# The order of the output projection's three parts, and where the last cached latents and the value weights are held, in a two-layer hybrid trunk

## The chip, the cores and the metric

The kernel runs on one core of one Trainium2 chip. The metric is the device time of one execution in microseconds (us), the median of several runs. The profile is of one further execution.

## The reference, cut to what matters

Two layers, each a SwiGLU, a mixer with three kinds of heads, and a second SwiGLU. 256 prompt tokens and 8 sample sequences of 8 new tokens go through together: 320 columns.

```python
x = x + 0.5 * swiglu(rms_norm(x, W['norm_ffn1'][l]), W['ffn1_wi'][l], W['ffn1_wo'][l])
p = rms_norm(x, W['norm_mix'][l]) @ W['w_in'][l]
...
o_hg, hg_s = hgrn2_mixer(p_hg, lbs[l], W['hg_norm'][l], hg_s0[l])
o_rw, rw_s, rw_sh = rwkv7_mixer(p_rw, rw_sh0[l], rw_s0[l], l, W)
o_mla = attend(l, q_nope, q_pe, c, k_pe)
o = jnp.concatenate([o_hg, o_rw, o_mla], axis=-1)      # 256 + 256 + 512 columns
x = x + o @ W['w_out'][l]
x = x + 0.5 * swiglu(rms_norm(x, W['norm_ffn2'][l]), W['ffn2_wi'][l], W['ffn2_wo'][l])
...
# the MLA attention of the samples, over 2048 cached positions in 16 pages of 128
s_past = jnp.einsum('bqhr,bkr->bhqk', q_lat, c_past) + jnp.einsum('bqhe,bke->bhqk', q_pe, kpe_past)
pr = jax.nn.softmax(s, axis=-1)
o_lat = jnp.einsum('bhqk,bkr->bqhr', pr[..., :P], c_past) + jnp.einsum('bhqk,bkr->bqhr', pr[..., P:], c)
o = jnp.einsum('bqhr,rhd->bqhd', o_lat, wuv)
```

## The kernel before, in words

Activations lie transposed: 128 features on the partitions, 320 tokens along a row, eight such tiles for the 1024 features (`xT`, and `oh`/`ol` for the mixer's output). Every dense product is made with operands split into a high and a low part (`split`: a cast on ACT, a subtraction on DVE) and three matmuls for each 128 x 128 block of weights (`block`, `dense`). Weights of the mixer come as a stream `wm` of chunks of four blocks in the order of their use; `_pack_mixer` lays them out by `OUT_PARTS`, so the stream follows any change of it. Four chunks can wait as loaded (`raw`), three as split (`w4`).

The mixer of a layer is written as generators that `weave` interleaves: `hg` (HGRN2), `prompt` (attention of the prompt), `sample` (attention of the samples), `w_out` (parts of the output projection). A generator yields the estimated time after which it may go on, or the name of an event that it waits for; `weave` keeps an estimate of PE's time (`self.pe`). This gives the order in which the program is written. A planner then lists the instructions of each engine and queue in order of time by its own costs, earlier instructions first where several are ready; `issue_after(i)` keeps an instruction behind `i` on its engine. On the chip every engine goes through its list in order.

`sample` handles the eight sequences in four pairs p. For each pair, `scores` multiplies queries with key pages (tag `ct`, five places of two pages), `values` multiplies the soft-max with latent pages (tag `cn`, five places of two pages) in four chunks of two halves (`hf`) of two sequences (`si`). While pair p has its values made, pair p+1 has its scores made; in the last pair (p = 3) there are values alone. Pages are loaded from SP's queue, one transfer of 128 KB for each. Then come the product with the new keys, the division by the sum (L988), two transposes, the copy into `qlat` (L994), and the product with the value weights `wuv`, which are loaded into two places of `cn` (L1000).

The output projection adds its result to `xT` (L613, L625) for eight column blocks m, part by part. `w_out` makes the parts [2, 3] (RWKV-7; waits for R0 and R1) and [4, 5] (half of MLA; waits for the end of `sample` and of `prompt`) within `weave`, and `mix_out` the last, [6, 7, 0, 1], after it, where each column block is followed by its share of the next norm. L293 is the line of all matmuls but transposes (L297), L434 and L435 the two instructions of every split.

Of the kernel before, what the change touches and what calls it, by code (L numbers as in the profile page):

```python
# [20 lines left out]
TP = 256  # L21
# [5 lines left out]
RANK = 256  # L27
# [11 lines left out]
LEVELS = [32, 16, 8, 4, 2, 1]  # L39
PACE = (0, 1.05)  # L40
ORDER_A = lambda fill, sample: (sample, fill)
ORDER_B = lambda prompt, sample: (sample, prompt)

LAG = 2.8
# [12 lines left out]
def _blocks(w):  # L57
    k, n = w.shape
    return w.reshape(k // 128, 128, n // 128, 128).transpose(2, 0, 1, 3).reshape(-1, 128, 128)
# [2 lines left out]
RW_TILES = [6, 2, 0, 4, 3, 1, 5]  # L62
HG_TILES = [2, 0, 4, 6, 3, 1, 5, 7]

OUT_PARTS = [(("R0", "R1"), [2, 3]), (("smp", "prompt"), [4, 5]), (None, [6, 7, 0, 1])]


def _perm(tiles):
    return np.concatenate([np.arange(j * 128, j * 128 + 128) for j in tiles])


def _stream(parts, n):
    b = np.concatenate(parts, 0)
    return b.reshape(-1, n, 128, 128).transpose(0, 2, 1, 3).reshape(-1, 128, n * 128)


def _pairs(b, K):

    return b.reshape(-1, 2, K // MBLK, MBLK, 128, 128).transpose(0, 2, 1, 3, 4, 5).reshape(-1, 128, 128)
# [7 lines left out]
def _pack_mixer(i, l):  # L87
# [10 lines left out]
    return _stream([_pairs(_blocks(mlt[:, :256]), KD), _blocks(mlt[:, 256:]), _blocks(qq), np.zeros((QPAD, 128, 128), wo.dtype), _blocks(rw[:, _perm(RW_TILES)]), _blocks(hg[:, _perm(HG_TILES)]),  # L98
                    *[_blocks(np.concatenate([wo[r * 128:r * 128 + 128] for r in p], 0)) for _, p in OUT_PARTS]], MBLK)

# [163 lines left out]
class Kern:  # L264
# [339 lines left out]
    def w_out(self):  # L604
        for wait, part in OUT_PARTS[:-1]:
            for e in wait:
                yield e
            ohs, ols = [self.oh[:, k, :] for k in part], [self.ol[:, k, :] for k in part]
            for m in range(KD):
                self.mark(f"w_out{self.l}")  # L610
                po = self.bank()[:, :T]
                yield from self.dense_steps(po, len(part), ohs, ols)
                self.nc.vector.tensor_tensor(out=self.xT[:, m, :], in0=po, in1=self.xT[:, m, :], op=ALU.add)  # L613
                if len(part) == 1:
                    yield 0

    def mix_out(self, l, fp, nxt):
        self.mark(f"mix_out{l}")
        part = OUT_PARTS[-1][1]
        ohs, ols = [self.oh[:, k, :] for k in part], [self.ol[:, k, :] for k in part]  # L620
# [230 lines left out]
    def sample(self):  # L851
        nc, l = self.nc, self.l
# [4 lines left out]
        ps = self.bank("pa")  # L857
# [3 lines left out]
        qlat = self.qlat  # L861
# [4 lines left out]
        def ready(name, n):  # L866
            f = feed[name]
            f[0] = max(f[0], f[1][f[2] - 3] if f[2] > 2 else 0.0) + n * (PACE[1] if f[2] < PACE[0] else 1.05)
            f[2] += 1
            return 0, f[0] + 2.2  # L870

        def pages(i, n):

            with self.tc.issue_after(self.gat[-8].ins) if len(self.gat) >= 8 else ExitStack():
                return nc.values_load_multi_w_load_instructions(
                    self.pti[0:1, i:i + n], engines=[mybir.EngineType.SP], min_val=0, max_val=NPOOL - 1,
                    skip_runtime_bounds_check_because="a page table names pages of the pool")[1]
# [44 lines left out]
        def exps(p, ch):  # L922
            m = mx[p]
            nc.scalar.activation(S[p, ch], S[p, ch], AF.Exp, bias=m[:, 5:6], scale=MLA_SCALE, accum_out=m[:, ch:ch + 1])  # L924

        def values(p, ch, po):
            r0 = ready("cn", 4)
            cns_ = []
            rs = []
            for si in range(2):  # L930
                i = (2 * p + si) * NPAGE + ch * 4
                rs.append(pages(i, 4))
            for hf in range(2):
                for si in range(2):
                    cn = self.s([128, 2, RANK], "cn", 5)
                    for pg in range(2):
                        r = rs[si][hf * 2 + pg]
                        self.gat.append(nc.sync.dma_start(cn[:, pg, :], self.ap["cn"][l, bass.ds(r, 1)].rearrange("a p c -> p (a c)")))
                    cns_.append(cn)
            yield 0, r0[1] - 1.5  # L940
            self.mark(f"sample{l}")
            if ch < 3:
                exps(p, ch + 1)
            pt = self.bank("pa")
            for pg in range(4):
                self.tr(pt[:, pg * 128:pg * 128 + 128], S[p, ch][:, pg * 128:pg * 128 + 128], idt)
            PT = self.s([128, 512], "PT", 2)
            nc.vector.tensor_copy(PT, pt)
            yield 0, max(self.pe + 1.2, r0[1])
            for hf in range(2):  # L950
                self.mark(f"sample{l}")
                for pg in (2 * hf, 2 * hf + 1):
                    for si in range(2):
                        self.mm(po[64 * si:64 * si + 64, :RANK], PT[:, pg * 128 + 64 * si:pg * 128 + 64 * si + 64],
                                cns_[2 * hf + si][:, pg % 2, :], start=ch == 0 and pg == 0, stop=False)
                feed["cn"][1].append(self.pe)
                if hf == 0:
                    yield ready("cn", 4)
# [4 lines left out]
        soft(0)  # L963
        yield 2.0
        for p in range(4):
            po = self.bank("pv")
            exps(p, 0)
            for ch in range(4):
                yield from values(p, ch, po)
                if p < 3:  # L970
                    yield from scores(p + 1, ch)
            exps(p, 4)
            nc.vector.tensor_reduce(out=mx[p][:, 6:7], in_=mx[p][:, 0:5], axis=AX.X, op=ALU.add)
            nc.vector.reciprocal(mx[p][:, 6:7], mx[p][:, 6:7])
            yield 0.6
            self.mark(f"sample{l}")
            pt = self.bank("pa")
            self.tr(pt[:64, :128], S[p, 4], idt)
            PN = self.s([64, 128], "PT", 2)
            nc.vector.tensor_copy(PN, pt[:64, :128])  # L980
            if p < 3:
                soft(p + 1)
            yield 0.8
            self.mark(f"sample{l}")
            for si in range(2):
                self.mm(po[64 * si:64 * si + 64, :RANK], PN[:, 64 * si:64 * si + 64], cns, start=False, stop=True)
            ol = self.s([128, RANK], "PT", 2)
            nc.vector.tensor_scalar(out=ol, in0=po[:, :RANK], scalar1=mx[p][:, 6:7], scalar2=None, op0=ALU.mult)  # L988
            yield 0.9
            self.mark(f"sample{l}")  # L990
            pt = self.bank("pa")
            for rt in range(2):
                self.tr(pt[:, rt * 128:rt * 128 + 128], ol[:, rt * 128:rt * 128 + 128], idt)
            nc.scalar.copy(qlat[:, 0:2, 2 * p:2 * p + 2, :, :].rearrange("p r s h t -> p r (s h t)"),  # L994
                           pt[:, :256].rearrange("p (r x) -> p r x", r=2))
            yield 2.0
        self.mark(f"sample{l}")
        wuv = [self.s([128, 512], "cn", 5) for rt in range(2)]
        for rt in range(2):
            nc.sync.dma_start(wuv[rt], self.ap["wuv"][l][:, rt * 512:rt * 512 + 512])  # L1000
        yield 4.0
        self.mark(f"sample{l}")
        for g in range(4):
            ps = self.bank("pa")
            for rt in range(2):
                for hh in range(2):
                    h = 2 * g + hh
                    self.mm(ps[64 * hh:64 * hh + 64, :64], wuv[rt][:, h * 64:h * 64 + 64], qlat[:, rt, :, h, :],
                            start=rt == 0, stop=rt == 1)
            self.split(ps[:, :64], self.oh[:, 4 + g, TP:], self.ol[:, 4 + g, TP:])  # L1010
        self.ev["smp"] = self.pe + 1.0


# [542 lines left out]
```

## Time and profile before

| | |
|---|---|
| median of 3 runs | 1659.08 us (1657.40 to 1660.34) |
| the profiled execution, its own time | 1657.07 us |
| span of its profile | 1655.1 us |
| busy: PE, its weight loads, DVE, ACT, POOL | 98%, 87%, 58%, 43%, 5% |
| mean granted clock | 0.993 |
| DMA | 260.82 MB, mean 158 GB/s |

The span runs from the first to the last instruction of the profile. Busy time is the union of an engine's instructions; a line of the timeline merges neighbours of a kind (xcount). An arrow in brackets gives the idle time just before and what ended it. The last pair's values and the end of the mixer lie at 550 to 606 us in layer 0 and at 1367 to 1420 us in layer 1.

### The profile page before, as it was taken

What the parts mean: (1) busy time and instruction counts of PE and PEld (TensorE: products, weight loads), DVE (VectorE), ACT (ScalarE), POOL (GpSimd) and SP (SyncE); (2) the same over time, 40 slices, a digit from 0 to 9 for tenths busy, and PEclk for the clock granted to TensorE, in tenths of its full rate; (3) what the DMA queues carried; (4) which work ended last, traced back from release to release, by engine and by line L of the source; (5) the groups of instructions that cost most, each with busy time, mean ns of one, the idle gap of its engine ahead of it and who ended that gap; (6) DMA issues with size and microseconds to landing.
All of it is one profiled execution on the core that took longest, in us unless ns stands there. A gap on an engine that the chain in (4) does not pass through costs nothing.

```text
span 1655.1 us, 33369 instructions
## 1 busy us (share of the span) xinstructions
PE 1615.0 (98%) x13138; PEld 1441.2 (87%) x13138; DVE 957.8 (58%) x1593; ACT 716.0 (43%) x1207; POOL 83.6 (5%) x118
## 2 busy tenths in 40 slices
PE   8999999999999899999999999999999999999998
PEld 8999998776657599999999999987766676999997
DVE  7555448853445585555465554479444665755543
ACT  6444434543353364444344443346333534544432
POOL 0000000200022000000000000012000310000000
PEclk9999999999999999999999999999999999999999
DMA  8444536646673464445445544365457644454442
GB/s 284 148 149 150 153 90 183 179 134 193 182 219 91 143 215 146 150 153 149 147 149 153 148 147 152 100 187 178 118 173 212 205 134 147 151 149 153 153 146 90
DMA packets 131899, 260.82 MB, mean 158 GB/s; under 512 B 17872, under 2 KB 76816, under 8 KB 131744
## 3 DMA queue, kind: packets, MB, share of 16 engines
q1 hardware_dynamic: 118912, 237.34, 47.5%
q10 hardware_dynamic: 12800, 21.30, 4.3%
q8 instruction: 103, 1.69, 0.4%
q0 software_dynamic: 32, 0.07, 0.1%
q14 instruction: 52, 0.43, 0.1%
HBM read 253.52 MB, written 4.47 MB: 156 GB/s over the span
## 4 chain that ended last, share of the span: by engine, by line
PE 88%; DVE 5%; ACT 3%; DMA 2%; issue 1%; SPq 1%; ACTq 0%; DVEq 0%
PE pd L293 33%; PE pr L293 31%; PE pa L293 18%; PE pv L293 4%; DVE w L435 1%; PE pa L297 1%; ACT S L924 1%; DMA cn<-in_cn 1%; DMA raw<-in_wm 1%; DMA ct<-in_ct 1%; DMA xT<-in_x 0%; DVE kS L458 0%; ACT w L434 0%; DVE rt L1073 0%; ACT L924 0%
## 5 line engine op out<-in xcount | busy, mean ns | idle before, releaser
L435 DVE TENSOR_TENSOR w<-raw,w 128x1024 fp32r<-128x1024 f32 (+1 forms) x390 | 412.6, 1060 | 320.1 <-ACT w L434 313.4
L434 ACT CAST w<-raw 128x1024 fp32r<-128x1024 f32 (+1 forms) x390 | 353.2, 910 | 420.5 <-PE pd L293 192.4
L293 PE MATMUL pd<-xh,w 128*128 128x320 f32 x1792 | 423.7, 316 | 8.3 <-ACT w L434 7.1
L293 PEld LDWEIGHTS pd<-xh,w 128*128 128x128 f32 x1792 | 305.2, 189 | 25.5 <-issue 11.4
L293 PE MATMUL pd<-xl,w 128*128 128x320 f32 x896 | 279.9, 314 | 0.0
L293 PE MATMUL pr<-xh,w 128*128 128x320 f32 x1056 | 240.2, 310 | 0.0
L293 PE MATMUL pa<-xh,w 128*128 128x320 f32 x896 | 201.7, 309 | 0.0
L293 PEld LDWEIGHTS pr<-xh,w 128*128 128x128 f32 x1056 | 178.3, 188 | 0.5
L293 PEld LDWEIGHTS pd<-xl,w 128*128 128x128 f32 x896 | 169.7, 189 | 4.9 <-issue 3.5
L293 PE MATMUL pr<-xl,w 128*128 128x320 f32 x528 | 162.5, 309 | 0.0
L293 PE MATMUL pd<-hh,w 128*128 128x320 f32 x704 | 158.2, 309 | 0.0
L293 PE MATMUL pr<-hh,w 128*128 128x320 f32 x704 | 158.2, 309 | 0.0
L293 PEld LDWEIGHTS pa<-xh,w 128*128 128x128 f32 x896 | 151.0, 188 | 0.0
L293 PE MATMUL pa<-xl,w 128*128 128x320 f32 x448 | 137.6, 309 | 0.0
L293 PE MATMUL pa<-ct,qlat 96*64 96x256 f32 x768 | 122.4, 391 | 2.6 <-ACT qlat L994 1.8
L293 PEld LDWEIGHTS pr<-hh,w 128*128 128x128 f32 x704 | 118.4, 188 | 0.0
L293 PEld LDWEIGHTS pd<-hh,w 128*128 128x128 f32 x704 | 118.4, 188 | 0.0
L293 PE MATMUL pr<-hl,w 128*128 128x320 f32 x352 | 108.8, 309 | 0.0
L293 PE MATMUL pd<-hl,w 128*128 128x320 f32 x352 | 108.8, 309 | 0.0
L482 ACT ACTIVATE fa<-fa 128x320 f32<-128x320 f32 x88 | 41.4, 472 | 134.7 <-DVE fa L481 134.7
L293 PEld LDWEIGHTS pr<-xl,w 128*128 128x128 f32 x528 | 99.1, 188 | 0.3
L293 PEld LDWEIGHTS pa<-ct,qlat 96*64 96x64 f32 x768 | 60.6, 137 | 38.4 <-issue 12.2
(388 smaller groups left out, 1996.6 us busy)
## 6 DMA issues: line engine op xcount, KB each, us to landing
raw<-in_wf SPq DMA_DIRECT2D x264, 512.0 KB, 3.6
ct<-in_ct SPq DMA_DIRECT2D x256, 144.0 KB, 3.0
cn<-in_cn SPq DMA_DIRECT2D x256, 128.0 KB, 2.3
raw<-in_wm ACTq DMA_DIRECT2D x76, 256.0 KB, 3.1
raw<-in_wm SPq DMA_DIRECT2D x50, 256.0 KB, 3.5
xT<-in_x SPq DMA_DIRECT2D x4, 320.0 KB, 6.8
wukt<-in_wukt SPq DMA_DIRECT2D x2, 576.0 KB, 5.5
S<-in_rws SPq DMA_DIRECT2D x4, 256.0 KB, 2.9
```

What stands on the lines that cost most here:

```text
L293: self.last = self.nc.tensor.matmul(out, w, x, start=start, stop=stop)
L297: self.nc.tensor.transpose(out, x, ident)
L434: self.cast = nc.scalar.copy(h, src).ins
L435: nc.vector.tensor_tensor(out=lo, in0=src, in1=h.bitcast(F32), op=ALU.subtract)
L482: nc.scalar.activation(a, a, AF.Silu)
L924: nc.scalar.activation(S[p, ch], S[p, ch], AF.Exp, bias=m[:, 5:6], scale=MLA_SCALE, accum_out=m[:, ch:ch + 1])
```

## The change

`OUT_PARTS` becomes [2, 3], [0, 1], and last [4, 5, 6, 7]. The second part waits for the events of both HGRN2 halves and for "end", which is set as the last half of the last values is written; its matmuls are kept behind the last value product (`self.held`). In the last pair the second half of each chunk loads its latents into places of `ct`, and so does `wuv`, which is asked for at the start of that pair. The four groups of the final sample product share one PSUM bank and one split.

```diff
-OUT_PARTS = [(("R0", "R1"), [2, 3]), (("smp", "prompt"), [4, 5]), (None, [6, 7, 0, 1])]
+OUT_PARTS = [(("R0", "R1"), [2, 3]), (("h0", "h1", "end"), [0, 1]), (None, [4, 5, 6, 7])]
...
             for m in range(KD):
                 self.mark(f"w_out{self.l}")
                 po = self.bank()[:, :T]
-                yield from self.dense_steps(po, len(part), ohs, ols)
+                with self.tc.issue_after(self.held) if "end" in wait else ExitStack():
+                    self.dense(po, len(part), ohs, ols)
+                yield 0
                 self.nc.vector.tensor_tensor(out=self.xT[:, m, :], in0=po, in1=self.xT[:, m, :], op=ALU.add)
-                if len(part) == 1:
-                    yield 0
...
-                    cn = self.s([128, 2, RANK], "cn", 5)
+                    cn = self.s([128, 2, RANK], "ct" if p == 3 and hf else "cn", 5)
...
                 self.mark(f"sample{l}")
+                if (p, ch, hf) == (3, 3, 1):
+                    self.ev["end"] = self.pe
                 for pg in (2 * hf, 2 * hf + 1):
...
+                self.held = self.last.ins
...
         for p in range(4):
+            if p == 3:
+                wuv = [self.s([128, 512], "ct", 5) for rt in range(2)]
+                for rt in range(2):
+                    nc.sync.dma_start(wuv[rt], self.ap["wuv"][l][:, rt * 512:rt * 512 + 512])
             po = self.bank("pv")
...
-        wuv = [self.s([128, 512], "cn", 5) for rt in range(2)]
-        for rt in range(2):
-            nc.sync.dma_start(wuv[rt], self.ap["wuv"][l][:, rt * 512:rt * 512 + 512])
-        yield 4.0
-        self.mark(f"sample{l}")
+        ps = self.bank("pa")
         for g in range(4):
-            ps = self.bank("pa")
             for rt in range(2):
                 for hh in range(2):
                     h = 2 * g + hh
-                    self.mm(ps[64 * hh:64 * hh + 64, :64], wuv[rt][:, h * 64:h * 64 + 64], qlat[:, rt, :, h, :],
+                    self.mm(ps[64 * hh:64 * hh + 64, g * 64:g * 64 + 64], wuv[rt][:, h * 64:h * 64 + 64], qlat[:, rt, :, h, :],
                             start=rt == 0, stop=rt == 1)
-            self.split(ps[:, :64], self.oh[:, 4 + g, TP:], self.ol[:, 4 + g, TP:])
+        self.split(ps[:, :256].rearrange("p (g t) -> p g t", g=4), self.oh[:, 4:8, TP:], self.ol[:, 4:8, TP:])
```

## Rows read from the trace of the kernel before

**Rows 1.** The page: span, and busy time of the engines.
```profile
span 1655.1 us, 33369 instructions
...
PE 1615.0 (98%) x13138; PEld 1441.2 (87%) x13138; DVE 957.8 (58%) x1593; ACT 716.0 (43%) x1207; POOL 83.6 (5%) x118
```

**Rows 2.** Windows: length, busy PE, PEld, DVE, ACT, POOL; clock, DMA share, GB/s.
```profile
545.00:550.00 5.00, 3.95 (x28) 2.72 (x24) 4.89 (x15) 4.38 (x11) 0.00 (x0) 1.00 0.50 151
...
1360.00:1365.00 5.00, 3.60 (x32) 2.57 (x30) 4.51 (x15) 2.66 (x6) 0.00 (x0) 1.00 0.64 179
```

**Rows 3.** Windows, end of the samples in layer 0, layer 1, and after it.
```profile
550.90:562.60 11.70, 11.69 (x79) 6.70 (x80) 6.61 (x17) 5.23 (x20) 0.00 (x0) 1.00 0.59 165
562.60:570.90 8.30, 6.13 (x44) 3.08 (x42) 2.56 (x9) 1.69 (x5) 0.00 (x0) 1.00 0.59 182
570.90:574.00 3.10, 2.05 (x22) 1.26 (x22) 0.53 (x2) 0.58 (x2) 0.00 (x0) 0.83 0.00 0
574.00:576.30 2.30, 2.30 (x15) 1.95 (x14) 0.40 (x2) 0.21 (x1) 0.00 (x0) 0.50 0.00 0
...
1379.60:1385.90 6.30, 5.27 (x35) 2.39 (x33) 2.38 (x8) 1.33 (x3) 0.00 (x0) 1.00 0.64 206
1385.90:1388.70 2.80, 1.67 (x23) 0.84 (x23) 0.53 (x2) 0.64 (x3) 0.00 (x0) 1.00 0.00 0
...
582.90:606.00 23.10, 23.10 (x158) 22.94 (x158) 20.24 (x38) 15.91 (x29) 0.00 (x0) 1.00 0.76 261
```

**Rows 4.** Timeline of PE, layer 0: start, us, instruction, count, idle before.
```profile
550.91 1.95 PE L293 MATMUL pv<-cn,PT 128*64 128x256 f32 x16
...
564.50 0.65 PE L293 MATMUL pv<-cn,PT 128*64 128x256 f32 x4 [0.52 <-DMA cn<-in_cn]
...
568.06 0.82 PE L293 MATMUL pd<-pPT,V 128*64 128x256 f32 x8
570.25 0.65 PE L293 MATMUL pv<-cn,PT 128*64 128x256 f32 x2 [1.37 <-DMA cn<-in_cn]
...
572.06 0.44 PE L297 MATMUL pa<-cf,PT 128*128 128x128 f32 x2 [0.59 <-DVE PT L988]
572.96 1.12 PE L293 MATMUL pa<-qlat,cn 128*64 128x64 f32 x16 [0.46 <-ACT qlat L994]
```

**Rows 5.** Timeline of PE, layer 1.
```profile
1380.63 1.26 PE L293 MATMUL pv<-cn,PT 128*64 128x256 f32 x6 [0.48 <-DMA cn<-in_cn]
...
1385.20 0.65 PE L293 MATMUL pv<-cn,PT 128*64 128x256 f32 x2 [0.55 <-DMA cn<-in_cn]
```

**Rows 6.** Timeline of SP's queue, layer 0, and its longest wait for the values.
```profile
540.00 4.50 SPq L938 DMA_DIRECT2D cn<-in_cn  x8
...
552.02 13.11 SPq L938 DMA_DIRECT2D cn<-in_cn  x21
565.23 0.85 SPq L1000 DMA_DIRECT2D cn<-in_wuv  x2
566.27 0.34 SPq L938 DMA_DIRECT2D cn<-in_cn  x1
...
SPq L938 <- PE pv L293: 12.1, 5, 6.9
```

**Rows 7.** The chain that ended last: 48 dense matmuls in a row (start, us).
```profile
25.27 7.04 PE pa L293 x48
```

**Rows 8.** Timelines of ACT and DVE at the samples' end; HGRN2's last splits.
```profile
572.54 0.37 ACT L994 COPY qlat<-pa 128x256 f32<-128x256 f32 x1 [3.23 <-PE pa L297]
...
571.52 0.48 DVE L988 TENSOR_SCALAR PT<-pv,smx 128x256 f32<-128x256 f32 x1 [1.76 <-PE pv L293]
...
569.34 0.42 DVE L435 TENSOR_TENSOR xl<-pd,xh 128x256 fp32r<-128x256 f32 x1 [1.26 <-ACT xh L434]
...
547.10 0.47 DVE L435 TENSOR_TENSOR xl<-EX,xh 128x320 fp32r<-128x320 f32 x1
```

**Rows 9.** Transfers into `cn` between 505 and 575.
```profile
DMA to landing us min/median/max: 1.9/2.1/3.9
```

## The prediction

> **What bounds the kernel now.** The page comes first: TensorE (PE) is busy for 1615.0 of a span of 1655.1 us [rows 1]. An edit is therefore worth what it changes in PE's 40 us without work, in the granted clock, or in the number of matmuls. This change leaves the matmuls as they are. Second, the windows, to find the idle time: the reader is to see that each layer has two thin places at the end of its mixer. The earlier one [rows 2] lies before the first values of the last sample pair, and nothing in the change touches the soft-max it waits for. The later one is where the change works [rows 3]: from 562.6 PE has work for 6.13 of 8.30 us, from 570.9 for 2.05 of 3.10 us; in layer 1 for 5.27 of 6.30 and 1.67 of 2.80 us. That is idle for 2.17, 1.05, 1.03 and 1.13 us, 5.38 us in all. After it PE is full (23.10 of 23.10 us, last row of the group). Third, PE's timeline, to see who ends each gap: landing latents (0.52, then 1.37 us; in layer 1 0.48 and 0.55), then the sample chain itself, the scaled sum (0.59 us) and the copy into `qlat` (0.46) [rows 4, 5]. Fourth, SP's timeline, to see why the last latents come so late [rows 6].
>
> **The change part by part, output order.** The output projection has 8 column blocks; a part with two row blocks has 8 x 2 x 3 = 48 matmuls, and 48 of this shape take 7.04 us [rows 7]. Before: 48 for [2, 3], 48 for [4, 5], 96 in `mix_out`. After: 48, 48 for [0, 1], 96. No work is added, and the weight stream is packed in the same order as it is used. What moves is what PE may do while the sample chain runs. Part [4, 5] needs the end of that chain; [0, 1] needs only HGRN2, whose last split in layer 0 ends at 547.6 [rows 8]. So 7.04 us of matmuls may now stand between the last value product and the end of the chain. The chain is the product with the new keys, the scale (0.48 us), two transposes, the copy into `qlat` (0.37 us), 32 small products and the split [rows 4, 8]. By the steps that the generators yield, the order is: one block of 0.88 us (7.04/8), the transpose, one block, the new keys' product, two blocks, two transposes, three blocks, the 32 products, the last block. Each gap (0.59, 0.46) has a block or more over it, so I take all of 1.05 and 1.13 us as gone. What is late next is the start of `mix_out`, which needs all of the MLA rows: a cast of 256 columns takes 0.37 us (the copy of that shape), its subtraction 0.42 us, with hand-overs about 0.9 us [rows 8]; over it lies the last block, 0.88 us. Cost 0 if that block is still there, 0.9 us a layer if not; I take 0.1, since the order above leaves it. DVE's eight additions and the casts of weights are as many as before. The order behind `held` adds no semaphore: it only places these matmuls in PE's list, and what stands behind them there is the sample chain (one block, 0.88 us, late at each of its steps, which the 7.04 us cover) and `mix_out`.
>
> **The clock.** From 574.0 to 576.3 the granted clock is 0.50, the lower of the two levels (1.2 GHz), and 0.83 in the 3.1 us before [rows 3]: 0.5 x 2.30 + 0.17 x 3.10 = 1.68 us lost. It fell after the idle stretch that ends with 1.37, 0.59 and 0.46 us without work; layer 1 has 0.55 and then 1.13 us idle and stays at 1.00. If the idle goes, so does the fall: between 0 and 1.68 us. As one layer of two shows it, I take half, 0.84.
> The Trainium skill (TensorE: Matmul & The Clock Gate, "Part 1: The HAM clock gate") says that the monitor runs freely, not from the kernel's start, so where the clock changes can differ from run to run. By that rule the 1.68 us is partly luck of the profiled run and the sum could lose its 0.84; by the row alone the whole 1.68 would be gained. The trace has two like stretches and one fall, which speaks for the rule.
>
> **Places for the last latents.** Each of the last pair's values has 16 tiles of two pages. Before, all share five places: two pages are asked for before 540 (32 less the 30 of the rows), eight from 540.00 to 544.5, and then SP waits 6.9 us, until the first products of the values (550.91) free places: 21 pages from 552.02 at the pace of the products [rows 4, 6]. After, half of them use `ct`, whose five places the keys no longer need, less two for `wuv`: eight tiles or 16 pages can be there early, 16 are left. The tiles of the last chunk's first half then stand in places freed two chunks earlier, so the waits of 0.52 and 0.48 us should go. The last tile is no better off: in both orders its place is freed by the last products of the chunk before. But before, its second page stood in SP's queue behind the two `wuv` transfers, which waited for a place of the value products (565.23), and it was asked for at 566.27 and landed 3.9 us later, the longest of the stretch; a page's median is 2.1 us [rows 6, 9]. Without them it can follow its first page, at about 565.1, and land near 567.3, not 570.2. What stays: from freeing to landing two issues of 0.33 us with their gaps, some 0.9, and 2.1 us, 3.0 in all; ahead of its use lies half a chunk of products (1.95/2 = 1.0 us) and whatever the prompt still has (its last eight products ran at 568.06 [rows 4]). So between 0 and 2.0 us a layer remains; I take 0.5, near the low end, since the prompt's matmuls last as long as the values.
>
> **Value weights early.** Two issues (0.85 us [rows 6]) and 0.5 MB move from the end to about 540, ahead of some of the last pair's latents on SP. The first ten pages were asked for by 544.5 and, with 2.1 us, landed by 546.6, 4.3 us ahead of their first use; that hides it. Without that cover it would cost up to about 2 us (0.5 MB at the 0.25 MB per us that DMA reaches in rows 3's last window). I take 0. The 4.0 that the generator yielded for them was program order, not time.
>
> **One split.** Four casts on ACT, each of 64 columns, become one of 256, about 0.37 us, and likewise on DVE 0.42 [rows 8]. Both engines wait for PE there, so 0; their end is counted above.
>
> **Sum.** 5.38 + 0.84 - 2 x 0.1 - 2 x 0.5 = 5.0 us. The profiled execution took 1657.07 us: 1655.1 of span and 2.0 around it. It gives 1652.1. The median of the three timed runs, 1659.08, lies 2.0 above the profiled one, so on that scale **1654.1**.
>
> **Rivals.** (B) The output matmuls fill the chain but the waits for latents stay, because the last tile's place comes free as late as before and the order on PE is planned, not dynamic. Gain 1.05 + 1.13 + 0.84 - 0.2 = 2.8: 1656.3. For it: the dependency of the last tile is the same; against it: the row at 566.27 shows that the `wuv` issues, not the place, held its page.
> (C) The latents come in time but the planner spends all of [0, 1] ahead of the chain, so that its gaps and the split stand bare in front of `mix_out`: the chain's 2.18 us stays, 0.9 a layer is added, the clock may still fall. Gain 2.17 + 1.03 - 1.0, less 1.8: 0.4, so about 1658.7. For it: each output matmul is ready as soon as it is held no more; against it: the chain's steps come before most blocks in program order.
> (D) Slower: three places in `ct` become a loop. Each second half of a chunk waits for the second half before it: 3.0 us less 1.0 us of own products, 2.0 us bare in three chunks, 6.0 a layer. Layer 0 then has 6.0 in place of 2.17 and loses 1.05 and 1.68 elsewhere (+1.1), layer 1 6.0 in place of 1.03, less 1.13 (+3.8): 4.9 slower, 1664.0. It decides from the point where the prompt's matmuls end before the second chunk of values. Against it: they run to 568.9, and values and prompt together keep PE at work for 17.8 of the 20 us before 570.9 (11.69 and 6.13, [rows 3]).
> (E) The planner merely places the same gaps elsewhere: 1659.
>
> **Chances.** Forecast 0.50, B 0.19, C 0.12, D 0.12, E 0.07. About 0.2% (3.3 us) is what a measurement of this kernel can tell from no change. Faster by more: 0.47 of the forecast's 0.50 and 0.08 of B's, 0.55. Slower: nearly all of D and a little of E, 0.12. Within: 0.33. The forecast alone runs from 1651.5 (all 5.38 and 1.68 gained, 7.06, and a little more) to 1656; with B, C and E the range is 1651 to 1660, which leaves out D and the far ends.
>
> **What would show it.** In the changed profile: output matmuls (`pd` from `xh` and `w`) between the last value products and the 32 small ones, and no idle over 0.3 us there; clock 1.00 through the end of both mixers; on SP the two `wuv` issues some 20 us earlier and the last page within 1 us of the page before it; waits of the value products for `cn` under 0.5 us a layer; the first `mix_out` matmul without a wait for the split. The prediction is wrong if a new wait for `ct` appears between the values' chunks, if the last block of [0, 1] ends before the 32 products, or if PE's idle in the two stretches falls by less than 3 us in all.

## The result, and the profile after

The changed kernel takes 1676.56 us (median of 11 executions, 1668.81 to 1684.49 but for one disturbed one, which is left out of the ratio); the kernel before, timed beside it, 1662.08 us (1657.40 to 1668.00). The ratio is 1.0081, 95% interval 1.0062 to 1.0100: slower, where 1654.1 was forecast. The profiled execution took 1677.72 us. The one of before (1657.07) lies at the fast end of its kernel's executions, so the two profiles differ by more than the medians do.

The page of the changed kernel, span and busy time, against [rows 1]:

```profile
span 1675.6 us, 33327 instructions
...
PE 1626.4 (97%) x13138; PEld 1440.7 (86%) x13138; DVE 954.3 (57%) x1587; ACT 713.8 (43%) x1201; POOL 83.8 (5%) x118
```

In these two profiles PE has as many matmuls as before, is idle for 49.2 us and not 40.1, and busy for 11.4 us more, at a mean granted clock of 0.988 and not 0.993. That difference of the clock is mostly luck of the two profiled executions: the mean over the timed executions is 0.990 before (75 in the experiments' rounds) and 0.989 after (10). The time of an execution multiplied by its mean clock is an estimate of what it would take at full clock. Its median is 1645.7 us before and 1657.6 after, so some 12 of the 14.5 us between the medians are not the clock's.

To find the place, the second view is VectorE's timeline, of which only the reciprocal of each norm is taken. Two of them bracket layer 1's mixer, first before, then after (start, duration, idle before):

```profile
1074.96 2.15 DVE L458 RECIPROCAL rstd<-rstd 128x320 f32<-128x320 f32 x1 [1.00 <-ACT rstd L457]
1421.66 2.15 DVE L458 RECIPROCAL rstd<-rstd 128x320 f32<-128x320 f32 x1 [0.61 <-ACT rstd L457]
```

```profile
1072.44 2.15 DVE L459 RECIPROCAL rstd<-rstd 128x320 f32<-128x320 f32 x1 [1.00 <-ACT rstd L458]
1443.17 2.15 DVE L459 RECIPROCAL rstd<-rstd 128x320 f32<-128x320 f32 x1 [1.58 <-ACT rstd L458]
```

The reader is to see that all is lost in layer 1: the first norm comes 2.5 us earlier than before, the second 21.5 us later. The stage between them grew from 346.7 to 370.7 us.

PE's timeline in layer 0, answering to [rows 4], and its windows, answering to [rows 3]:

```profile
555.51 1.18 PE L294 MATMUL pv<-cn,PT 128*64 128x256 f32 x6 [0.75 <-DMA cn<-in_cn]
...
557.90 1.08 PE L294 MATMUL pv<-ct,PT 128*64 128x256 f32 x6 [0.65 <-DMA ct<-in_cn]
...
564.21 0.42 PE L294 MATMUL pd<-xh,w 128*128 128x320 f32 x1
...
568.60 0.38 PE L298 MATMUL pa<-cf,PT 128*128 128x128 f32 x2
568.91 0.87 PE L294 MATMUL pd<-pPT,V 128*64 128x256 f32 x8
...
574.03 0.42 PE L294 MATMUL pd<-xh,w 128*128 128x320 f32 x1 [0.51 <-ACT pPT L839]
```

```profile
554.80:564.20 9.40, 6.36 (x30) 2.28 (x30) 0.48 (x2) 0.00 (x0) 0.00 (x0) 1.00 0.65 186
564.20:573.50 9.30, 9.30 (x85) 7.37 (x84) 6.52 (x13) 2.36 (x6) 0.00 (x0) 1.00 0.22 58
...
1290.00:1305.00 15.00, 13.38 (x47) 6.58 (x47) 3.80 (x11) 7.83 (x20) 2.01 (x2) 0.66 0.46 160
...
1375.00:1380.00 5.00, 5.00 (x22) 2.23 (x18) 0.00 (x0) 0.37 (x1) 0.00 (x0) 0.50 0.59 177
1380.00:1385.20 5.20, 2.25 (x11) 1.58 (x10) 1.69 (x4) 3.69 (x11) 0.00 (x0) 0.50 0.64 197
1385.20:1401.40 16.20, 13.32 (x75) 5.73 (x74) 2.58 (x6) 0.16 (x2) 0.00 (x0) 0.97 0.60 175
```

The sample chain is covered as forecast (9.30 of 9.30 us, clock 1.00). But ahead of it PE has values alone and waits for latents: 6.36 of 9.40 us. In `pd` no matmul of the prompt stands between 549 and 568.9; before, they ran among the values until 568.88 [rows 4]. Now the prompt comes last, and PE waits 0.51 us for it at 574.03. Layer 1 shows the same, and more, with the lower level of the clock in two places (0.66 in the window from 1290, 0.50 in those from 1375):

```profile
1371.18 0.62 PE L294 MATMUL pa<-ct,qlat 96*64 96x256 f32 x2 [1.18 <-DMA ct<-in_ct]
...
1383.29 1.97 PE L298 MATMUL pa<-cf,S 128*128 128x128 f32 x8 [2.95 <-ACT S L925]
...
1401.39 0.41 PE L294 MATMUL pd<-xh,w 128*128 128x320 f32 x1
...
1406.10 0.87 PE L294 MATMUL pd<-pPT,V 128*64 128x256 f32 x8
```

The first row is a wait for *key* pages of the last pair, which no part of the change touches. SP's timelines in layer 1, before and after, say why they are late:

```profile
1342.69 3.78 SPq L895 DMA_DIRECT2D ct<-in_ct  x5
...
1347.13 0.32 SPq L895 DMA_DIRECT2D ct<-in_ct  x1
1347.55 5.12 SPq L1459 DMA_DIRECT2D o_hgs<-S  x2
1353.46 0.90 SPq L895 DMA_DIRECT2D ct<-in_ct  x2
```

```profile
1354.21 6.65 SPq L1464 DMA_DIRECT2D o_hgs<-S  x2
1362.76 0.34 SPq L380 DMA_DIRECT2D raw<-in_wm  x1
1364.49 3.12 SPq L940 DMA_DIRECT2D cn<-in_cn  x6
1368.34 5.47 SPq L896 DMA_DIRECT2D ct<-in_ct  x8
```

Before, six of the eight key pages stand ahead of HGRN2's state outputs; after, all eight stand behind them, a weight fetch and six latent pages. The planner has written another list for layer 1. Compared by the tiles of each matmul, the two traces have the same order on TensorE from 620 us, through both FFNs, up to matmul 9030 of 13138 (at 1175.3 us before, 1174.4 after), and then differ in RWKV-7's stage, whose code is the same. So the study had two questions: what the new list costs, and what the change is worth under one list.

### The profile page after: what moved, and what is told of

It reads as the page before. It is cut to its first block, busy times and chain, and to the rows that moved or that the text cites. A ratio compares the mean times of both kernels' runs of the same rounds, so it can differ in the third digit from the quotient of the medians.

```text
span 1675.6 us, 33327 instructions
## 1 busy us (share of the span) xinstructions
PE 1626.4 (97%) x13138; PEld 1440.7 (86%) x13138; DVE 954.3 (57%) x1587; ACT 713.8 (43%) x1201; POOL 83.8 (5%) x118
## 5 line engine op out<-in xcount | busy, mean ns | idle before, releaser
L294 PE MATMUL pd<-xh,w 128*128 128x320 f32 x1792 | 422.2, 315 | 12.8 <-ACT w L435 7.4
```

What stands on the lines that cost most here:

```text
L294: self.last = self.nc.tensor.matmul(out, w, x, start=start, stop=stop)
```

## The experiments

All were timed in five rounds beside the kernel before, whose median in these rounds was 1661.75 to 1662.99 us; a difference from the kernel before goes by its median in the same rounds. "Keys ahead" or "behind" tells the kind of layer 1's list by the mark just shown. Stage 0 runs from the second pair's scaled sum in layer 0 (466.7 in the kernel before) to the norm at 1075, stage 1 from there to the next mixer's norm at 1422; "slow" is half the time at the lower clock in stage 1, which is the most that it can have cost. Stages are those of one profiled execution, which need not be a middling one: that of before took 5.0 us less than its median, that of e1 7.5 more, that of e10 4.8 more.

| kernel | median us | ratio to before, 95% | stage 0 | stage 1 (slow) | keys |
|---|---|---|---|---|---|
| before | 1662.08 | | 608.3 | 346.7 (1.7) | ahead |
| after | 1676.56 | 1.0081 (1.0062 to 1.0100) | 608.1 | 370.7 (15.4) | behind |
| e1 | 1661.17 | 0.9997 (0.9977 to 1.0017) | 610.7 | 358.8 (10.2) | ahead |
| e2 | 1676.20 | 1.0082 (1.0061 to 1.0104) | 608.0 | 367.2 (15.4) | behind |
| e3 | 1657.63 | 0.9969 (0.9952 to 0.9987) | 609.4 | 345.6 (3.4) | ahead |
| e4 | 1647.40 | 0.9917 (0.9895 to 0.9940) | 603.6 | 342.3 (3.4) | ahead |
| e5 | 1673.79 | 1.0072 (1.0047 to 1.0097) | 607.9 | 366.9 (10.2) | late |
| e6 | 1660.48 | 0.9986 (0.9969 to 1.0003) | 609.5 | 351.5 (8.5) | ahead |
| e7 | 1665.43 | 1.0018 (1.0003 to 1.0032) | 608.0 | 354.8 (1.7) | ahead |
| e8 | 1665.40 | 1.0012 (0.9995 to 1.0030) | 603.7 | 360.7 (11.9) | behind |
| e9 | 1673.55 | 1.0075 (1.0056 to 1.0094) | 610.6 | 361.3 (10.2) | behind |
| e10 | 1663.94 | 1.0019 (1.0001 to 1.0038) | 608.3 | 359.9 (10.2) | ahead |
| e11 | 1661.20 | 1.0002 (0.9986 to 1.0018) | 604.0 | 357.5 (5.1) | behind |

**e1 and e2: the whole change in one layer alone.**

```diff
-        part = OUT_PARTS[-1][1]
+        part = OUT_PARTS[l][-1][1]     # the new parts in one layer, the old in the other
...
-                    cn = self.s([128, 2, RANK], "cn", 5)
+                    cn = self.s([128, 2, RANK], "ct" if l in PLACE and p == 3 and hf else "cn", 5)
```

> The whole change in layer 1 alone; layer 0 is as before, and with it the planned order of layer 1 up to the last pair's values. Replanning theory (the loss comes from layer 1's mixer being ordered anew, because the planner reaches it at another planned time): no loss from that, only the end of layer 1, so within 4 us of before. Theory of a direct cost (the last pair's stage itself is what became slower): the loss of 13 to 20 us stands in layer 1's tail, so 10 us or more slower.

> The whole change in layer 0 alone; layer 1's code is as before. Replanning theory: the order of layer 1 on PE and SP still comes out other than before, so most of the loss is here, 8 to 15 us slower, and it stands in layer 1 between the RWKV-7 and the HGRN2 stage. Theory of a direct cost: within 4 us of before, as layer 0's own tail in the changed kernel ended level with before.

The change in layer 1, where all was lost, costs nothing; in layer 0 alone, it costs all of it, and the time goes in layer 1, which that kernel leaves as it was (stage 1 367.2, stage 0 608.0). The theory of the new list holds, the direct costs fall.

**e3 and e4: the held blocks in another PSUM tag.**

```diff
-                po = self.bank()[:, :T]
+                po = self.bank("pr" if "end" in wait else "pd")[:, :T]
```

> As the first run of this set, but the held output matmuls take their PSUM banks from pr (three, free once HGRN2 is done) and not from pd, where two held blocks keep both banks from the prompt's heads. Bank theory: the prompt's products stand beside the last values again, so 2 to 4 us faster than before the change and 2 to 5 us faster than the run with pd. If the places in ct are what makes the values wait: no difference between the two runs, and waits for latents of over 2 us stay.

> The change in both layers with pr banks for the held matmuls. Bank theory alone: 5 us faster than before, in each layer idle of under 1 us behind 551 and 1367. Replanning theory: layer 0's tail gains 2 to 5 us, but layer 1's order is another again, and what it costs there, between -3 and +15 us, cannot be told beforehand; it would stand between the RWKV-7 and the HGRN2 stage of layer 1.

By the code, `pd` has two banks, handed out in the order of the program. The first two held blocks take both when they are written, and may not run before the last value product; so whatever of the prompt is written behind them waits as long. With `pr` (three banks, HGRN2's, which is done by then) PE's timeline of e4 in layer 0 has the prompt between the values again:

```profile
553.93 0.87 PE L296 MATMUL pd<-pPT,V 128*64 128x256 f32 x8
554.73 1.13 PE L296 MATMUL pd<-kT,qT 96*128 96x256 f32 x4
...
558.79 0.65 PE L300 MATMUL pd<-cf,wuv 128*128 128x128 f32 x4
...
561.80 0.65 PE L296 MATMUL pv<-cn,PT 128*64 128x256 f32 x4 [0.39 <-DMA cn<-in_cn]
...
565.69 0.41 PE L296 MATMUL pr<-xh,w 128*128 128x320 f32 x1
```

e3 has e1's list on SP and is 3.5 us faster by the medians, as the bank theory had it (2 to 5); its waits for latents in layer 1 are 0.92 us (0.25 + 0.67). e4 is 15.6 us faster than the kernel before, and beats both kernels. That is three times what the bank theory gave it (5); how much of it is the banks, e11 asks.

**e5: the state outputs off SP's queue.**

```diff
-        nc.sync.dma_start(self.ap["o_hgs"][l][:, hp * 512:hp * 512 + 512], ...)
+        (nc.gpsimd if l else nc.sync).dma_start(self.ap["o_hgs"][l][:, hp * 512:hp * 512 + 512], ...)
```

> The change in both layers, as timed at a ratio of 1.008, but layer 1's two HGRN2 sample state outputs are issued on GpSimd's queue and no more on SP's; TensorE's list and the rest of SP's list are those of the changed kernel. SP-block theory: in the changed kernel the last pair's key pages stand in SP's list behind these two outputs, which wait for the states; without them the pages are asked for some 6 us earlier, the waits for keys and for the scores of the last pair in layer 1 (1.2 and 2.95 us) go, and perhaps the clock's fall at 1372.7 (13.65 us at half clock, up to 6.8 us lost): 4 to 10 us faster than the changed kernel, so 1666 to 1673, ratio to before 1.002 to 1.006. TensorE-order theory: the loss comes from what stands behind what on TensorE (the output blocks that wait for RWKV's split at 1285 to 1295), SP's list only follows: within 3 us of the changed kernel, ratio 1.006 to 1.010.

Against the changed kernel 2.8 us by the medians, with overlapping intervals. SP's timeline of e5 shows that the next entries of its list wait almost as long, the fetch for a free place and the pages for the value products:

```profile
1359.62 0.33 SPq L382 DMA_DIRECT2D raw<-in_wm  x1
1361.35 3.11 SPq L941 DMA_DIRECT2D cn<-in_cn  x6
1365.18 5.47 SPq L898 DMA_DIRECT2D ct<-in_ct  x8
```

The waits that were to go stayed: 1.31 us for keys and 2.95 for the last pair's scores, against 1.18 and 2.95 in the changed kernel. The gain is under the 4 us that the SP-block theory needed. The outputs were in the way, but are not the price. The place of the key pages is a mark of the list, no more.

**e6: one split in layer 0, nothing else.**

```diff
-            self.split(ps[:, :64], self.oh[:, 4 + g, TP:], self.ol[:, 4 + g, TP:])
+        self.split(ps[:, :256].rearrange("p (g t) -> p g t", g=4), ...)    # layer 0 alone
```

> The kernel before with one edit in layer 0 alone: one split of 256 columns for the samples' rows instead of four of 64, valued at 0 in the prediction. No other part of the change is in. TensorE's list differs from that of before by a few places at layer 0's end and then in many places in layer 1's RWKV-7 stage, whose code is untouched; on SP one RWKV-7 state output stands 42 rows later. Replanning theory: layer 0's end takes the same time within 1 us, and whatever the total moves (I expect between 6 faster and 8 slower, and more than 2 either way) stands in layer 1. Direct-cost theory (an edit moves only the stretch that it touches): total within 1.5 us of before and layer 1 as long as before within 1 us.

Layer 1's list changes, and the total stays within what can be measured (the 2 us that I expected did not come). Another list need not be a slower one.

**e7 and e8: the two parts apart,** the output order with `pr` banks, and the places with early value weights and one split, both layers each.

```diff
 e7, of e4:
-                    cn = self.s([128, 2, RANK], "ct" if p == 3 and hf else "cn", 5)
+                    cn = self.s([128, 2, RANK], "cn", 5)
 e8, of the changed kernel:
-OUT_PARTS = [(("R0", "R1"), [2, 3]), (("h0", "h1", "end"), [0, 1]), (None, [4, 5, 6, 7])]
+OUT_PARTS = [(("R0", "R1"), [2, 3]), (("smp", "prompt"), [4, 5]), (None, [6, 7, 0, 1])]
```

> Output order alone, in both layers, with the held blocks in the pr banks; last latents, value weights and splits as before. If the held blocks are what gains: 8 to 13 us faster than before (all but 3 us of the 15.6 that both parts gave together). By the prediction's own terms (1.05 + 1.13 + 0.84 - 0.2): 2.8 us faster. If the places for the latents are what gains: within 3 us of before.

> Places in ct for the last latents, early value weights and the one split, in both layers; output order as before (no held blocks). By the prediction's own terms (2.17 + 1.03 - 1.0): 2.2 us faster. SP-block theory: here too layer 1's state outputs stand on SP ahead of the last pair's eight key pages, so layer 1's last pair is late as in the changed kernel: 4 to 10 us slower than before. TensorE-order theory: no output block stands behind RWKV's split here, so within 3 us of before.

Each part alone is 3.5 us slower by the medians (e8's interval reaches 1), the two together 15.6 faster: totals don't add when each version draws its own list. None of e7's expectations came, and e8's result lies on the edge between its two theories and decides neither.

Stage 0 does tell the parts apart: 608.0 with the order, 603.7 with the places. PE's timeline of e7 shows the waits for latents as before, and a new wait for weights in `mix_out`; in e8 the prompt's last transposes and products come behind the last values and leave no gap in the sample chain, without any held block:

```profile
568.63 0.65 PE L296 MATMUL pv<-cn,PT 128*64 128x256 f32 x2 [1.51 <-DMA cn<-in_cn]
...
601.42 0.41 PE L296 MATMUL pr<-xh,w 128*128 128x320 f32 x1 [1.19 <-ACT w L437]
```

```profile
569.15 0.66 PE L300 MATMUL pd<-cf,wuk 128*128 128x128 f32 x4
569.81 0.44 PE L300 MATMUL pa<-cf,PT 128*128 128x128 f32 x2
570.31 0.87 PE L296 MATMUL pd<-pPT,V 128*64 128x256 f32 x8
571.01 1.10 PE L296 MATMUL pa<-qlat,ct 128*64 128x64 f32 x32
572.58 0.56 PE L296 MATMUL pd<-xh,w 128*128 128x320 f32 x2 [0.47 <-ACT xh L437]
```

e8's list has the keys behind the outputs, and PE's timeline shows the longest wait for them of all:

```profile
1362.41 1.08 PE L296 MATMUL pa<-ct,qlat 96*64 96x256 f32 x2 [3.83 <-DMA ct<-in_ct]
```

**e9, e10 and e11: the list alone.** One or two copies on VectorE that nobody reads, after layer 0's mixer.

```diff
             self.norm_tile(m, *nxt)
         self.norm_close()
+        if l == 0:
+            scr = self.t(self.xp, [128, T], "scr")
+            for _ in range(2):          # e9: on the kernel before; e10, e11: one copy
+                self.nc.vector.tensor_copy(scr, self.xT[:, 7, :])
```

> The kernel before, and nothing of the change, with two copies of 128x320 on VectorE put in after layer 0's mixer (a scratch tile that nobody reads, about 0.4 us each, VectorE is busy for 60% of that stretch). TensorE's list is that of before up to its row 7744, in layer 1's RWKV-7 stage, and differs behind it; on SP the key pages of layer 1's last sample pair now stand behind the HGRN2 state outputs, as in the changed kernel. Replanning theory: layer 0 and the two FFNs as before within 1 us (the norm behind the second FFN at 1075.0 within 1), layer 1's mixer 8 to 16 us longer, total 1670 to 1678, ratio 1.005 to 1.010. Theory that the edits themselves cost the time: two hidden copies, total within 2 us of before.

> The changed kernel with one such copy at the same place. TensorE's list is that of the changed kernel up to its row 7539 (layer 0 and both FFNs the same) and differs in layer 1; on SP all eight key pages of the last pair stand ahead of the state outputs. Replanning theory: 8 to 16 us faster than the changed kernel with more work in it, 1660 to 1668, ratio to before 0.999 to 1.004 (the prompt is still shut out by the held blocks' banks in both layers, which keeps it from reaching the 1647 of the pr banks). Theory that the edits themselves cost the time: as the changed kernel, 1675 to 1678, ratio 1.008.

> The change in both layers with the held blocks in the pr banks (ratio 0.992 when run without the copy), with one such copy at the same place. TensorE's list is the same up to row 7541; in layer 1 it differs, and on SP the last pair's eight key pages stand behind the state outputs, as in the changed kernel. If the 15.6 us of the pr banks were mostly a lucky list for layer 1: 8 to 15 us slower than without the copy, 1655 to 1662, ratio 0.996 to 1.001. If the gain is the banks' own: within 3 us of 1647, ratio 0.990 to 0.994.

e9 is the kernel before with two copies of 0.32 us. VectorE's reciprocals show layer 0 and the FFNs as before (1075.41 against 1074.96) and layer 1 14.6 us longer; SP's list has turned:

```profile
1075.41 2.15 DVE L461 RECIPROCAL rstd<-rstd 128x320 f32<-128x320 f32 x1 [1.00 <-ACT rstd L460]
1436.73 2.15 DVE L461 RECIPROCAL rstd<-rstd 128x320 f32<-128x320 f32 x1 [0.61 <-ACT rstd L460]
```

```profile
1351.02 0.34 SPq L1482 DMA_DIRECT2D o_hgs<-S  x1
...
1355.72 0.35 SPq L1482 DMA_DIRECT2D o_hgs<-S  x1
...
1359.03 5.08 SPq L902 DMA_DIRECT2D ct<-in_ct  x7
```

All of that is as the replanning theory had it. e10 is the changed kernel with one copy more, and 12.6 us faster for it, as expected. In SP's timeline its keys are ahead:

```profile
1346.05 5.94 SPq L902 DMA_DIRECT2D ct<-in_ct  x8
...
1359.37 6.66 SPq L1482 DMA_DIRECT2D o_hgs<-S  x2
```

Medians by version and kind of list:

| | keys ahead | keys behind | difference |
|---|---|---|---|
| before | 1662 | 1673.6 (e9) | 11.8 |
| the change, `pd` | 1663.9 (e10) | 1676.6 | 12.6 |
| the change, `pr` | 1647.4 (e4) | 1661.2 (e11) | 13.8 |

e11 answers the question that e4 left: one copy takes away 13.8 of its 15.6 us, so most of that was a lucky list, as the first of its expectations said. With that copy the `pr` kernel is level with the kernel before (0.9986 to 1.0018).

Read across, in these three pairs the list is worth 12 to 14 us with nothing else changed but a copy or two. Part of that is the clock: at full clock, by the estimate given with the result, the three differences are 6.4, 6.0 and 13.1 us. Read down, the change as made comes out 2 to 3 us slower under either kind, and with `pr` banks 12 to 15 faster. That the change itself does this is not shown, for lists of one kind are not the same list: e4 and e7 both have `pr` banks and keys ahead and lie 18 us apart, and e8 with keys behind is level with e7. What the parts give is seen in stage 0 alone: there e10 and e11 have TensorE's order of the kernels that they were made from, and repeat their times (608.3 and 608.1, 604.0 and 603.6).

## Why the prediction was wrong

**The step that failed** is one that the sum made without a line of its own: that a difference of two mixers' ends, 5.0 us in all, is the difference of the kernels, so that whatever lies outside [rows 2 to 6] stays put. The prediction knew that "the order on PE is planned, not dynamic" and used it only within the stretch. Rival E gave the planner a chance of 0.07 and a price of about zero (the same gaps, elsewhere). Its price is about 12 us, in a stage 500 us later. Of e9's 14.6 us in stage 1, up to 8.5 are lower clock (10.2 less 1.7), and PE's idle time is 6.6 more (19.4 against 12.8); of the 24.0 between the profiles of before and after, up to 13.65 are lower clock, and the idle time is 7.0 more (19.8).

**Places.** "I take 0.5, near the low end, since the prompt's matmuls last as long as the values": this cover was taken away by the change itself, whose held blocks keep `pd`. Waits for latents in layer 0 were 3.1 us (0.75 + 0.65 + 0.15 + 0.59 + 0.45 + 0.50), more than the 2.17 before. Where the prompt keeps its banks, 0.5 was near: 0.8 in e4 (0.39 + 0.18 + 0.24), 0.8 in e8 (0.15 + 0.68). So the point from which rival D decides was reached, the prompt gone before the second chunk of values; but its loop of three `ct` places cost 1.15 us (0.65 + 0.50), not 6.0, and the waits for `cn` more (1.94).

**Output order.** Right as far as it went: in layer 0 both gaps of the chain, 1.05 us, are gone. But it cost what its banks hold, and the 1.05 us was not its own: with the places alone (e8) the prompt's work covers the chain too. The start of `mix_out`, taken at 0.1 us, waits 0.47 us for the split in e4, e8 and e11.

**Clock.** Right in kind, too small: I took half of 1.68 us. The five profiles in which layer 0's end is as before (or has the one split alone) all show the lower level of 1.2 GHz near 570 us, for 3.4 to 6.8 us, so 1.7 to 3.4 lost at most; the eight with the change there, or with its order or its places alone, show none. Two windows from 570 to 578, of e9 and e10:

```profile
570.00:578.00 8.00, 7.32 (x50) 6.07 (x51) 2.56 (x8) 1.84 (x6) 0.00 (x0) 0.57 0.00 0
```

```profile
570.00:578.00 8.00, 7.49 (x75) 6.12 (x74) 5.52 (x13) 4.63 (x14) 0.00 (x0) 1.00 0.22 64
```

The Trainium skill (TensorE: Matmul & The Clock Gate, "Part 1: The HAM clock gate") has the monitor running freely, so that the point of a change varies. Where this fall begins does vary here, from 105.2 to 106.3 us behind the first mark of stage 0; that there is one does not (five profiles of five), and I let the rule halve a term that these profiles bear out whole.

**Value weights and one split.** At their place 0, as taken (two issues at 535.04 and 539.13, no wait behind them). The split is also an edit that turns layer 1's list (e6), which no step had.

**Layer 0 as a whole.** Forecast 2.17 + 1.05 - 0.6 + 0.84 = 3.5 us. Stage 0 takes 608.3 to 610.7 in the five kernels with layer 0's mixer end as before or with one split. With `pr` banks it takes 603.6 and 604.0, 4.3 to 4.7 less than in the profile that the forecast used; with `pd` 607.9 to 608.3 in four kernels, 0 to 0.4 less. That the 4.3 to 4.7 lie near the 3.5 is in part luck, for the terms don't add as the sum had it. The places alone take 603.7 (e8): in that profile they bring the latents, the cover of the chain and the clock together, and the order adds nothing to them. The order alone takes 608.0 (e7): it covers the chain, but waits 2.2 us for latents (0.73 + 1.51) and 1.2 for weights. What stays open is which matmuls of layer 1's list cost most: e5 ruled one candidate out, and the list was not taken apart further.

## What to carry to other kernels

Where a planner orders the program, lay the two instruction lists side by side over their whole length before valuing an edit: a difference behind the edit is a term of the sum, here 12 us beside one of 5. Judge an edit under several lists (a harmless operation draws another), and take what it gives in each, not one median against one. An instruction that is held back holds its buffers from the place where it is written: give held work a tag that nobody else is waiting for. And where two parts of an edit fill the same gap, run each alone before adding their terms: here one of them had it all.

## What the runs showed that was not expected

The granted clock sets the spread of a kernel's executions: the changed kernel took 1668.81 us at a mean of 0.993 and 1684.49 at 0.984, and 0.009 of 1676 us is 15 of these 15.7 us. Time multiplied by clock stays within 1656.7 to 1659.4 us in its ten executions. Slack of a few us on PE can be dear twice, as idle time and as the lower level after it, as at the end of layer 0. In layer 1's mixer the lists with keys behind lost up to 5.1 to 15.4 us to the lower level, those with keys ahead up to 1.7 to 10.2; the two ranges overlap, so this alone doesn't tell the lists apart.
